# Forming the gate's token mixes in streams of their own, and loading them from DRAM in both halves

## The chip, the cores and the metric

The kernel runs on one core of one Trainium2 chip. The metric is the device time of one execution in microseconds (us). The time before is the median of three runs. A profile is one further execution, taken with the hardware profiler; it has its own time.

## The reference, cut to what matters

Two decoder layers work on 512 tokens of 1024 channels. Layer 0 is an RWKV-7 time mixing with a SiLU gate, layer 1 a differential attention; each ends with a small gated embedding. Only layer 0's input side matters here:

```
x_prev = jnp.pad(xn, ((0, 0), (1, 0), (0, 0)))[:, :-1]
xmix = xn[None] + (x_prev - xn)[None] * mu[:, None, None, :]
rkvg = jnp.einsum('cbsd,cde->cbse', xmix[:4], w_in)
r, k, v, g = rkvg[0], rkvg[1], rkvg[2], rkvg[3]
...
_, y = lax.scan(step, state0, (r, decay, k, v, kk, a))
...
y = y.reshape(B, S, D).astype(xn.dtype) * jax.nn.silu(g)
return y @ w_out
```

Each of r, k, v and the gate g has a mix of its own: the normalised tokens blended with the tokens shifted by one. The mix is multiplied with a 1024 x 1024 weight. r, k and v feed the scan; g is needed only behind it.

## The kernel before

**Tiles.** Channels lie on the 128 partitions in 8 tiles `d`. Every operand of a dense product is split in two float32r parts, high and low, and a product takes three matmuls of 128x512 (`mm3`, L284, L285 and L286: here called a triple). A weight of 1024x1024 is used in two halves `hf` of 512 output channels. One half of one projection (`dense_m`) is 8 tiles `d` by 4 output blocks `e`, so 32 triples. Weights arrive by DMA (`w_load`, two buffers RAW) and are split by `w_split`: a cast to the high part on ScalarE or VectorE (L269), a subtraction for the low part on GpSimd or VectorE (L317).

**Mixes.** The 8 mixes of a projection are formed from the resident x by `mix`: ScalarE scales x into PSUM (L529), VectorE adds the shifted token (L531), ScalarE casts the high part (L535), VectorE subtracts the low part (L537). ScalarE then issues a store of the mix to DRAM (`mD`, L541, 512 KB). The first half that uses a projection takes the mix as formed; the second half loads it from `mD` on SyncE's queue (L523). At most two mixes of each parity of `d` are held at once (`MT`).

**Order of the dense work.** `ORDER` runs the halves as r0, k0, v0, r1, k1, v1, p0, g0, g1, p1 (p is the layers' embedding). Thus the gate's mixes are formed when g0 is at hand, after v1.

**The recurrence.** The scan runs in chunks of 64 tokens, for two groups of heads (g = 0 and 1; eight chunks c each, `recur`). Ahead of it stand, for each group, Gram matrices (`gram`, L971 and L980) and, for each pair of chunks-of-128, a triangular inverse (`inverse`): 31 steps of a multiply and an add on VectorE (L1038, L1041), transposes (L1029, L1047, L1062), and two batches of 64 small matmuls (L1074, L1088). The recurrence itself is a chain TensorE, ScalarE or VectorE copy, TensorE (L1175, L1188, L1216), with the state's update on VectorE (L1228, L1231). Dense triples stand between these steps as filler. `finish` (L1259 and on) normalises a block and multiplies it with the gate; behind it layer 0's output projection `out0` begins.

**What sets the order.** The whole program is a set of Python generators ("streams"). A planner (`Streams`) runs them against a table of costs, priorities and buffer counts while the program is built, and so writes a fixed order of instructions for TensorE, VectorE, ScalarE and GpSimd. It also chooses the engine where a step names two. On the chip each engine runs its list in order, and waits where an operand isn't there. SyncE's queue issues its DMAs in the order in which the planner came to them. `R` is a ring of 4 KB buffers per partition, `H` one of 2 KB.

Of the kernel before, what the change touches and what calls it, by code (L numbers as in the profile page):

```python
# [8 lines left out]
F32 = mybir.dt.float32  # L9
F32R = mybir.dt.float32r  # L10
AF = mybir.ActivationFunctionType
ALU = mybir.AluOpType
# [3 lines left out]
P = 128  # L16
D = 1024
S = 512
NT = D // P
# [11 lines left out]
V_G, V_MU, V_W0, V_A0, V_KK, V_KA, V_LB, V_G1, V_GKV = 0, 1, 7, 8, 9, 10, 11, 12, 13  # L31
# [5 lines left out]
FIRST = [(k, h) for n, (k, h) in enumerate(ORDER) if k not in [x for x, _ in ORDER[:n]]]  # L37
# [3 lines left out]
N_WT, N_MT, N_RAW = 8, 2, 2  # L41
# [1 line left out]
WLP, WP = 6, 7  # L43
XLP = (6, 0.5)
LO2P = (3, 3)
MIXP = (4, 5)
DECP = (3, 3.5)
EVP = {"v": 1.5, "r": 4, "k": 3, "g": 3}
GRP, OPP, RECP, FINP = (5, 2.5), (4, 4), (0.3, 0.3), (7.5, 7.6)
# [152 lines left out]
def yoco_kernel(ctx: ExitStack, tc: tile.TileContext, I, out):  # L202
    nc = tc.nc
    k = Core(tc, ctx)
# [3 lines left out]
    def pool(name, bufs=1, **kw):  # L208
        return tc.tile_pool(name=name, bufs=bufs, **kw)

    dram = ctx.enter_context(pool("dram", space=bass.MemoryType.DRAM))
    N_R, N_H = 44 - N_RAW, 11
    gD = dram.tile([NT, P, S], F32, name="gD")
    vcD = dram.tile([NB, P, D], F32, name="vcD")
    hD = dram.tile([NB, P, D], F32, name="hD")
# [1 line left out]
    mD = dram.tile([4, NT, P, 2, S], F32, name="mD")  # L217
# [12 lines left out]
    def bank(tag):  # L230
        return T(pp, [P, 512], "p", bufs=8)

    def R(shape, dt=F32):
        return T(ring, shape, "R", dt, bufs=N_R)
# [4 lines left out]
    sc = Streams(dict(NBUF, R=N_R, H=N_H, WT=N_WT, RAW=N_RAW) | {("MT", par): N_MT for par in range(2)})  # L239
# [31 lines left out]
    def vcol(v, t):  # L271
        return vec[:, v, t : t + 1]
# [22 lines left out]
    def w_load():  # L295
        for key, src, _ in wants:
            yield "take", "RAW", 1
            RAW[key] = T(raws, [P, 2, S], "RAW", bufs=N_RAW)
            yield "DMA!", 1.7
            nc.sync.dma_start(RAW[key], src)  # L300
            yield "set", ("load",) + key

    def w_split():
        yield "wait", ("norms",)
        for key, _, scale in wants:
            yield "wait", ("load",) + key
            for u in range(2):
                yield "take", "WT", 1
                yield "take", "R", 1, True
                d = 2 * key[-1] + u  # L310
                f, t = RAW[key][:, u], R([P, 2, S], F32R)
                hi, lo = t[:, 0], t[:, 1]
                if scale is None:
                    yield "ACT/DVE+", (0.52, 0.34)
                    copy(hi, f)
                    yield "Pool+/DVE+!", (1.25, 0.6)
                    ENG[sc.eng].tensor_sub(lo, f, hi.bitcast(F32))  # L317
                else:
                    g = vcol(scale, d)
                    yield "ACT", 0.62  # L320
                    nc.scalar.activation(hi, f, AF.Copy, scale=g)  # L321
                    yield "DVE+!", 0.67
                    nc.vector.scalar_tensor_tensor(lo, f, g, hi.bitcast(F32), ALU.mult, ALU.subtract)  # L323
                W[key[:-1] + (d,)] = (hi, lo)
                yield "set", ("W",) + key[:-1] + (d,)
            yield "free", "RAW", 1
# [95 lines left out]
    MIX = {"r": 0, "k": 1, "v": 2, "g": 3}  # L422
# [83 lines left out]
    def x_at(d):  # L506
        return xh[d // 2][:, d % 2, :]

    mixes = {}

    def mix(key, hf, par):

        c = MIX[key]
        for d in range(par, NT, 2):
            yield "wait", ("xh", d)
            yield "take", ("MT", par), 1
            yield "take", "R", 1, True
            mixes[key, hf, d] = t = R([P, 2, S], F32R)
            h, l = t[:, 0], t[:, 1]
            if (key, hf) not in FIRST:  # L520
                yield "wait", ("kept", key, d)
                yield "DMA", 1.7
                nc.sync.dma_start(t.bitcast(F32), mD[c, d])  # L523
                yield "set", ("mix", key, hf, d)
                continue
            yield "take", "pw", 1
            m = bank("pw")
            yield "ACT", 0.57
            nc.scalar.activation(m, x_at(d), AF.Copy, scale=omm[:, c, d : d + 1])  # L529
            yield "DVE", 0.67  # L530
            nc.vector.scalar_tensor_tensor(  # L531
                m[:, 1:], x_at(d)[:, 0 : S - 1], vcol(V_MU + c, d), m[:, 1:], ALU.mult, ALU.add
            )
            yield "ACT", 0.48
            nc.scalar.copy(h, m)  # L535
            yield "DVE", 0.6
            nc.vector.tensor_sub(l, m, h.bitcast(F32))  # L537
            yield "free", "pw", 1
            yield "set", ("mix", key, hf, d)
            yield "ACT!", 0.06  # L540
            nc.scalar.dma_start(mD[c, d], t.bitcast(F32))  # L541
            yield "set", ("kept", key, d)

    def mix_all(par):
        for key, hf in MIXES:
            yield from mix(key, hf, par)
        yield "free", "R", 2


# [134 lines left out]
    omm = T(ax, [P, 4, NT], "omm")  # L684
# [227 lines left out]
        sc.add(lora2(g), LO2P[g])  # L912
    for par in range(2):
        sc.add(mix_all(par), MIXP[par])
    sc.add(w_load(), WLP)
    sc.add(w_split(), WP)
    sc.add(fill(), 8)
# [1053 lines left out]
```

## Time and profile before

| what | value |
|---|---|
| median of three runs | 807.28 us (805.05 to 807.47) |
| the profiled execution's own time | 804.08 us |
| its span in the trace | 802.3 us |
| TensorE busy | 757.8 us, 94% of the span |
| VectorE busy | 594.5 us, 74% |
| ScalarE busy | 460.1 us, 57% |
| GpSimd busy | 184.9 us, 23% |
| mean DMA rate | 180 GB/s |

The span is the time from the first to the last instruction in the trace; the remaining 1.78 us lie around it. Matmuls overlap and their ends are modelled, so a busy TensorE is not TensorE at its peak.

### The profile page before, as it was taken

To read this page: it belongs to the slowest core of one execution; us is meant where nothing else is said; L and a number is where in the kernel's file an instruction comes from. 1 tells how busy PE (TensorE), PEld (TensorE's weight loads), DVE (VectorE), ACT (ScalarE), POOL (GpSimd) and SP (SyncE) were. 2 spreads that over 40 slices of the span, in tenths; PEclk is the share of its full clock that TensorE was granted. 3 is DMA by queue.
4 is the path that set the end of the run, shared out by engine and by line. 5 is a ranking of instruction groups with operands and counts; after the bars stand their busy time and mean duration, and the time that the engine had idled before them with its cause. 6 is when DMAs were issued, how large, how long until landed. Compare 5 with 4: busy or idle time off the path is not lost.

```text
span 802.3 us, 13875 instructions
## 1 busy us (share of the span) xinstructions
PE 757.8 (94%) x5016; PEld 607.2 (76%) x5016; DVE 594.5 (74%) x1360; ACT 460.1 (57%) x1091; POOL 184.9 (23%) x208
## 2 busy tenths in 40 slices
PE   6898999997999869899999999999999999999996
PEld 3576678875778657788788888887888888888884
DVE  2999999987869798798767685456875668835844
ACT  3789754668747566766444565333764567743431
POOL 2416404422313303874301010000000002100000
PEclk9999999999999969999999999999999999999998
DMA  8586676822436646847257334588943434224702
GB/s 322 195 262 232 215 263 230 296 93 94 138 100 224 246 186 221 266 155 242 99 184 263 131 110 151 185 289 235 298 164 105 113 83 133 83 75 157 259 5 105
DMA packets 65525, 144.60 MB, mean 180 GB/s; under 512 B 6448, under 2 KB 27184, under 8 KB 65456
## 3 DMA queue, kind: packets, MB, share of 16 engines
q1 hardware_dynamic: 42672, 108.06, 40.3%
q10 hardware_dynamic: 22784, 35.66, 12.9%
q8 instruction: 39, 0.64, 0.3%
q14 instruction: 30, 0.25, 0.1%
HBM read 105.94 MB, written 37.75 MB: 179 GB/s over the span
## 4 chain that ended last, share of the span: by engine, by line
PE 70%; DVE 15%; ACT 7%; DMA 5%; issue 2%; SPq 0%; ACTq 0%; POOL 0%; DVEq 0%; POOLq 0%
PE p L284 17%; PE p L286 17%; PE p L285 16%; PE p L1175 3%; DVE p L1041 2%; PE p L1775 2%; PE p L1188 2%; DVE H L1038 2%; ACT R L269 2%; PE p L971 1%; DVE p L531 1%; PE p L1740 1%; PE p L1216 1%; DVE R L537 1%; PE p L1739 1%
## 5 line engine op out<-in xcount | busy, mean ns | idle before, releaser
L284 PE MATMUL p<-R,R 128*128 128x512 f32 x800 | 327.9, 410 | 6.8 <-ACT H L860 4.0
L285 PE MATMUL p<-R,R 128*128 128x512 f32 x800 | 314.2, 393 | 3.4 <-DVE R L537 3.4
L286 PE MATMUL p<-R,R 128*128 128x512 f32 x800 | 314.4, 393 | 0.0
L284 PEld LDWEIGHTS p<-R,R 128*128 128x128 f32 x800 | 151.2, 189 | 41.2 <-ACT H L860 5.2
L286 PEld LDWEIGHTS p<-R,R 128*128 128x128 f32 x800 | 151.1, 189 | 33.4 <-DVE R L1305 0.4
L285 PEld LDWEIGHTS p<-R,R 128*128 128x128 f32 x800 | 151.6, 190 | 31.8 <-DVE R L537 5.3
L317 POOL TENSOR_TENSOR R<-RAW,R 128x512 fp32r<-128x512 f32 x48 | 64.9, 1357 | 163.4 <-ACT R L269 119.5
L269 ACT CAST R<-RAW 128x512 fp32r<-128x512 f32 x110 | 65.8, 619 | 19.5 <-DMA RAW<-in_w_k 8.0
L317 DVE TENSOR_TENSOR R<-RAW,R 128x512 fp32r<-128x512 f32 x92 | 64.3, 710 | 12.1 <-ACT R L269 10.8
L323 DVE SCALAR_TENSOR_TENSOR R<-RAW,vec,R 128x512 fp32r<-128x512 f32 x64 | 46.6, 748 | 18.1 <-ACT R L321 17.8
L321 ACT ACTIVATE R<-RAW,vec 128x512 fp32r<-128x512 f32 x64 | 44.6, 720 | 19.3 <-DMA RAW<-in_b_w_in 12.6
L1751 ACT ACTIVATE H<-p,mx 128x128 f32<-128x128 f32 (+3 forms) x64 | 33.4, 528 | 19.9 <-DVE mx L1748 17.9
L1384 POOL TENSOR_TENSOR hr<-hm,half 128x1 f32<-128x1 f32 x16 | 10.4, 649 | 147.7 <-DVE hm L1382 147.7
L1744 DVE CUSTOM_DVE_ANT_0 p<-p,cmask 128x128 f32<-128x128 f32 (+3 forms) x64 | 31.2, 523 | 13.6 <-PE p L1740 13.3
L1041 DVE TENSOR_TENSOR p<-p,H 128x126 f32<-128x126 f32 (+22 forms) x124 | 32.6, 263 | 4.3
L280 POOL TENSOR_TENSOR orr<-orm,half 128x4 f32<-128x4 f32 x8 | 8.8, 1102 | 105.8 <-DVE orm L278 92.3
L1038 DVE TENSOR_TENSOR H<-p,R 128x126 f32<-128x126 f32 (+22 forms) x124 | 30.8, 248 | 1.3
L1521 DVE SCALAR_TENSOR_TENSOR R<-H,R 128x512 f32<-128x512 f32 x16 | 11.1, 691 | 24.3 <-ACT H L1514 22.5
L1514 ACT ACTIVATE H<-p 128x512 f32<-128x512 f32 x16 | 9.5, 596 | 31.0 <-PE p L286 31.0
L1443 ACT COPY R<-p 128x512 f32<-128x512 f32 x16 | 9.4, 588 | 30.9 <-PE p L286 30.8
L531 DVE SCALAR_TENSOR_TENSOR p<-R,vec,p 128x511 f32<-128x511 f32 x32 | 23.7, 748 | 4.5 <-ACT p L529 4.4
L529 ACT ACTIVATE p<-R,omm 128x512 f32<-128x512 f32 x32 | 22.1, 692 | 7.4 <-DVE R L980 2.0
(226 smaller groups left out, 1263.7 us busy)
## 6 DMA issues: line engine op xcount, KB each, us to landing
mD<-R ACTq DMA_DIRECT2D x32, 512.0 KB, 3.3
R<-mD SPq DMA_DIRECT2D x32, 512.0 KB, 5.7
RAW<-in_ple_gate SPq DMA_DIRECT2D x16, 512.0 KB, 3.7
RAW<-in_kv_w SPq DMA_DIRECT2D x16, 512.0 KB, 3.6
RAW<-in_b_w_in SPq DMA_DIRECT2D x16, 512.0 KB, 4.4
R<-bD ACTq DMA_DIRECT2D x24, 256.0 KB, 4.8
R<-in_x SPq DMA_DIRECT2D x8, 512.0 KB, 6.1
RAW<-in_w_r SPq DMA_DIRECT2D x8, 512.0 KB, 3.9
```

Of the source, the lines that this page charges most:

```text
L269: (nc.scalar.copy if sc.eng == "ACT" else ENG[sc.eng].tensor_copy)(dst, src)
L284: nc.tensor.matmul(ps, ah, bh, start=first, stop=False)
L285: nc.tensor.matmul(ps, ah, bl, start=False, stop=False)
L286: nc.tensor.matmul(ps, al, bh, start=False, stop=last)
L317: ENG[sc.eng].tensor_sub(lo, f, hi.bitcast(F32))
L321: nc.scalar.activation(hi, f, AF.Copy, scale=g)
L323: nc.vector.scalar_tensor_tensor(lo, f, g, hi.bitcast(F32), ALU.mult, ALU.subtract)
L531: nc.vector.scalar_tensor_tensor(m[:, 1:], x_at(d)[:, 0 : S - 1], vcol(V_MU + c, d), m[:, 1:], ALU.mult, ALU.add)
L1038: ve.tensor_mul(tmp[:, 0:m, 0:w], bc(xs[:, s_ : s_ + 1, 0:w], [P, m, w]), bc(nb[:, s_ + 1 : 32, s_ : s_ + 1], [P, m, w]))
L1041: ve.tensor_add(xs[:, s_ + 1 : 32, 0:w], xs[:, s_ + 1 : 32, 0:w], tmp[:, 0:m, 0:w])
L1744: nc.vector.tensor_tensor_reduce(scs[m][:, 0:n], scs[m][:, 0:n], cmask[:, S - n : S], 1.0, -3.0e38, ALU.add, ALU.max, mx[:, m : m + 1])
L1751: nc.scalar.activation(E[m][:, 0:n], scs[m][:, 0:n], AF.Exp, bias=mx[:, m : m + 1], scale=0.125, accum_out=sm[:, m : m + 1])
```

## The change

The first-half branch of `mix` becomes a function, `mixed`. For the projections in `AHEAD` (the gate alone) two new streams, `mix_ahead`, one for each parity of `d`, call it once the second half of the keys (k1) is done on TensorE. Each mix is formed in a ring buffer, stored to `mD`, and the buffer is given back; after the last one the place of x is given back as well, which `mix_all` no longer does. Both halves of g load their mixes from `mD`. The new streams have priority 6; the ring gains one buffer of 4 KB, and `H` loses two of 2 KB.

```
-MIXP = (4, 5)
+MIXP = (4, 5, 6)
+AHEAD = ("g",)
...
-    N_R, N_H = 44 - N_RAW, 11
+    N_R, N_H = 45 - N_RAW, 9
...
+    def mixed(key, d, t):
...
     def mix(key, hf, par):
...
-            if (key, hf) not in FIRST:
+            if key in AHEAD or (key, hf) not in FIRST:
                 yield "wait", ("kept", key, d)
                 yield "DMA", 1.7
-                nc.sync.dma_start(t.bitcast(F32), mD[c, d])
...
+                nc.sync.dma_start(t.bitcast(F32), mD[MIX[key], d])
+            else:
+                yield from mixed(key, d, t)
             yield "set", ("mix", key, hf, d)
...
     def mix_all(par):
         for key, hf in MIXES:
             yield from mix(key, hf, par)
+
+    def mix_ahead(par):
+
+        yield "wait", ("dense", "k", 1)
+        for key in AHEAD:
+            for d in range(par, NT, 2):
+                yield "take", "R", 1, True
+                yield from mixed(key, d, R([P, 2, S], F32R))
+                yield "free", "R", 1
         yield "free", "R", 2
...
     for par in range(2):
         sc.add(mix_all(par), MIXP[par])
+        sc.add(mix_ahead(par), MIXP[2])
```

The planner's order moves all over layer 0's first part. Three places follow. In the changed kernel the lines have other numbers: L521 and L525 are before's L531 and L537, L270 is L269, L1241 and L1244 are L1228 and L1231, L1051 and L1054 are L1038 and L1041, L285 to L287 are L284 to L286, L1188 is L1175.

VectorE, in the first group's recurrence, at the state's update of chunk 2 (`R_1691`), before: keys' steps stand ahead of it and the keys' norms behind.

```order
L866 TENSOR_TENSOR R_1840<-H_2109,R_1840 128x4x2x64
L868 TENSOR_TENSOR R_1475<-H_2109,R_1475 128x4x128
L1228 TENSOR_TENSOR R_1691<-R_1691,p_2119 64x4x64
L1231 TENSOR_TENSOR R_1691<-R_1691,pcall_99 64x4x64
L1228 TENSOR_TENSOR R_1691<-R_1691,p_2119 64x4x64
L1231 TENSOR_TENSOR R_1691<-R_1691,pcall_99 64x4x64
L722 SCALAR_TENSOR_TENSOR R_1840<-H_2109,der_96,R_1840 128x4x128
```

The same place in the changed kernel (the state is `R_1716`, the gate's mixes read x from `R_116` and `R_118`):

```order
L521 SCALAR_TENSOR_TENSOR p_2114<-R_116,vec_87,p_2114 128x511
L521 SCALAR_TENSOR_TENSOR p_2124<-R_116,vec_87,p_2124 128x511
L1241 TENSOR_TENSOR R_1716<-R_1716,p_2135 64x4x64
L525 TENSOR_TENSOR R_1994<-p_2114,R_1994 128x512
L1244 TENSOR_TENSOR R_1716<-R_1716,pcall_99 64x4x64
L1241 TENSOR_TENSOR R_1716<-R_1716,p_2135 64x4x64
L1244 TENSOR_TENSOR R_1716<-R_1716,pcall_99 64x4x64
L525 TENSOR_TENSOR R_1995<-p_2124,R_1995 128x512
L521 SCALAR_TENSOR_TENSOR p_2200<-R_118,vec_87,p_2200 128x511
```

All 16 VectorE steps of the gate's mixes now stand from just ahead of chunk 2's update to just behind chunk 5's in the first group's recurrence.

VectorE, at the end of the second group's first inverse (`p_2586`) and the start of its second (`p_3050`), before:

```order
L1041 TENSOR_TENSOR p_2586<-p_2586,H_2579 128x16
L531 SCALAR_TENSOR_TENSOR p_3157<-R_167,vec_87,p_3157 128x511
L1047 STREAM_TRANSPOSE R_3172<-p_2586 128x1024
L1029 STREAM_TRANSPOSE R_3186<-H_3005 128x1024
L1058 SCALAR_TENSOR_TENSOR H_3180<-R_3172,rowm_104,H_3180 128x32x16
L1038 TENSOR_TENSOR H_3007<-p_3050,R_3186 128x31
```

The same in the changed kernel (the two inverses are `p_2776` and `p_3010`): the second begins while the first still has 13 steps to go, and no mix is among them.

```order
L1042 STREAM_TRANSPOSE R_3123<-H_2993 128x1024
L1051 TENSOR_TENSOR H_2758<-p_2776,R_2895 128x13x10
L1054 TENSOR_TENSOR p_2776<-p_2776,H_2758 128x13x10
L1051 TENSOR_TENSOR H_2995<-p_3010,R_3123 128x31
L1054 TENSOR_TENSOR p_3010<-p_3010,H_2995 128x31
L1051 TENSOR_TENSOR H_2758<-p_2776,R_2895 128x12x10
L1054 TENSOR_TENSOR p_2776<-p_2776,H_2758 128x12x10
```

All eight L531 and L537 of the gate stood among the second group's Gram matrices and inverses; now the two inverses alternate there.

TensorE, at the first matmuls of the second group's recurrence (L1175), before. The triples are those of the gate's first half, tile d = 7 (mix `R_3253`, weight `R_3037`); the first of its four blocks stands ahead.

```order
L286 MATMUL p_2994<-R_3131,R_2981 128x512
L284 MATMUL p_2933<-R_3253,R_3037 128x512
L285 MATMUL p_2933<-R_3253,R_3037 128x512
L286 MATMUL p_2933<-R_3253,R_3037 128x512
L1175 MATMUL p_3382<-R_2637,R_2467 64x64 x2
L1175 MATMUL p_3382<-R_2637,R_2468 64x64 x2
```

The same in the changed kernel: the triples are those of the gate's second half, tile d = 2 (mix `R_3274`, weight `R_3162`).

```order
L287 MATMUL p_3390<-R_3243,R_3152 128x512
L285 MATMUL p_3311<-R_3274,R_3162 128x512
L286 MATMUL p_3311<-R_3274,R_3162 128x512
L287 MATMUL p_3311<-R_3274,R_3162 128x512
L1188 MATMUL p_3486<-R_2755,R_2567 64x64 x2
L1188 MATMUL p_3486<-R_2755,R_2568 64x64 x2
```

Counted over the whole list, 237 triples stand ahead of this place before and 249 now. At the last matmul of the second group's recurrence the counts are 296 and 305. From the output projection on, the list of TensorE is nearly the same in both.

## Rows read from the trace of the kernel before

**Rows 1.** The page: span, busy time and share by engine, granted clock in 40 slices.

```profile
span 802.3 us, 13875 instructions
...
PE 757.8 (94%) x5016; PEld 607.2 (76%) x5016; DVE 594.5 (74%) x1360; ACT 460.1 (57%) x1091; POOL 184.9 (23%) x208
...
PEclk9999999999999969999999999999999999999998
```

**Rows 2.** Windows by stretch: length, busy PE, PEld, DVE, ACT, POOL; PEclk, DMA, GB/s.

```profile
172.00:245.00 73.00, 67.36 (x834) 52.26 (x832) 56.30 (x108) 50.99 (x137) 17.09 (x26) 0.98 0.32 104
244.50:308.50 64.00, 53.45 (x421) 41.78 (x422) 56.50 (x161) 42.16 (x98) 18.45 (x19) 0.89 0.61 218
308.50:383.00 74.50, 72.39 (x842) 57.66 (x839) 63.26 (x134) 45.34 (x119) 46.26 (x50) 1.00 0.68 220
383.00:470.00 87.00, 86.70 (x405) 71.03 (x405) 62.28 (x111) 44.77 (x94) 10.84 (x12) 1.00 0.47 162
470.00:802.00 332.00, 322.54 (x1614) 269.85 (x1612) 208.43 (x527) 165.84 (x420) 31.09 (x33) 0.99 0.48 153
```

**Rows 3.** Waits of TensorE, 244.5 to 308.5 us: us in total, times, longest.

```profile
PE p L1074 <- DVE H L1062: 5.0, 1, 5.0
PE p L971 <- DVE R L537: 2.9, 1, 2.9
```

**Rows 4.** Waits of VectorE, 172 to 245 us.

```profile
DVE H L269 <- ACT H L269: 5.3, 3, 3.1
DVE R L866 <- ACT H L860: 2.9, 1, 2.9
```

**Rows 5.** Groups by line, 240.5 to 300 us: busy us, mean ns, idle before.

```profile
L531 DVE SCALAR_TENSOR_TENSOR p<-R,vec,p 128x511 f32<-128x511 f32 x8 | 6.0, 748 | 4.0 <-ACT p L529 4.0
...
L537 DVE TENSOR_TENSOR R<-p,R 128x512 fp32r<-128x512 f32 x8 | 5.5, 681 | 0.0
...
L535 ACT CAST R<-p 128x512 fp32r<-128x512 f32 x8 | 4.7, 587 | 6.1 <-DVE p L531 5.9
```

**Rows 6.** Timeline of TensorE, first and last recurrence steps of the second group.

```profile
302.00 0.86 PE L1175 MATMUL p<-R,R 128*64 128x64 f32 x16
...
382.15 0.69 PE L1175 MATMUL p<-R,R 128*64 128x64 f32 x16
```

**Rows 7.** Windows: r's second half, g's first half, a dense stretch; columns as Rows 2.

```profile
121.40:145.40 24.00, 24.00 (x121) 19.68 (x121) 22.86 (x78) 10.20 (x28) 11.89 (x13) 1.00 0.78 272
261.70:306.80 45.10, 34.55 (x295) 26.64 (x294) 38.59 (x112) 28.69 (x75) 10.51 (x10) 0.85 0.57 209
500.00:520.00 20.00, 20.00 (x90) 16.53 (x89) 9.30 (x14) 5.56 (x10) 0.95 (x1) 1.00 0.52 180
```

**Rows 8.** Groups by line, whole run: the weights' low part on GpSimd and VectorE.

```profile
L317 POOL TENSOR_TENSOR R<-RAW,R 128x512 fp32r<-128x512 f32 x48 | 64.9, 1357 | 163.4 <-ACT R L269 119.5 <-issue 28.7 <-DVE R L269 3.9
...
L317 DVE TENSOR_TENSOR R<-RAW,R 128x512 fp32r<-128x512 f32 x92 | 64.3, 710 | 12.1 <-ACT R L269 10.8
```

**Rows 9.** Groups by line, 172 to 245 us: small copies on VectorE.

```profile
L269 DVE COPY H<-p 64x256 f32<-64x256 f32 x4 | 1.7, 425 | 5.6 <-ACT H L269 5.3 <-PE p L1188 0.3
...
L269 DVE COPY H<-R 32x128 f32<-32x128 f32 x6 | 1.3, 216 | 0.1
```

**Rows 10.** Tile mD, 100 to 160 us: loads of mixes and time to landing.

```profile
L523 SPq DMA_DIRECT2D R<-mD x15: 319/422/562, 106.7 to 153.2; - x15
...
DMA to landing us min/median/max: 2.7/5.8/8.6
```

**Rows 11.** Line L1231, the state's update: duration ns min/median/max.

```profile
L1231 DVE TENSOR_TENSOR R<-R,pcall x24: 409/422/1340, 176.2 to 376.7; 64x256 f32<-64x256 f32 x24
```

More of the change, by code (lines that the diff above doesn't have):

```diff
@@ L509, in yoco_kernel @@
     mixes = {}
+    def mixed(key, d, t):
+        c = MIX[key]
+        h, l = t[:, 0], t[:, 1]
+        yield "take", "pw", 1
+        m = bank("pw")
+        yield "ACT", 0.57
+        nc.scalar.activation(m, x_at(d), AF.Copy, scale=omm[:, c, d : d + 1])
+        yield "DVE", 0.67
+        nc.vector.scalar_tensor_tensor(m[:, 1:], x_at(d)[:, 0 : S - 1], vcol(V_MU + c, d), m[:, 1:], ALU.mult, ALU.add)
+        yield "ACT", 0.48
+        nc.scalar.copy(h, m)
+        yield "DVE", 0.6
+        nc.vector.tensor_sub(l, m, h.bitcast(F32))
+        yield "free", "pw", 1
+        yield "set", ("mixed", key, d)
+        yield "ACT!", 0.06
+        nc.scalar.dma_start(mD[c, d], t.bitcast(F32))
+        yield "set", ("kept", key, d)
     def mix(key, hf, par):
-        c = MIX[key]
         for d in range(par, NT, 2):
@@ L518, in mix @@
             mixes[key, hf, d] = t = R([P, 2, S], F32R)
-            h, l = t[:, 0], t[:, 1]
-            if (key, hf) not in FIRST:
+            if key in AHEAD or (key, hf) not in FIRST:
                 yield "wait", ("kept", key, d)
                 yield "DMA", 1.7
-                nc.sync.dma_start(t.bitcast(F32), mD[c, d])
[L524 to L538, printed above, removed]
+                nc.sync.dma_start(t.bitcast(F32), mD[MIX[key], d])
+            else:
+                yield from mixed(key, d, t)
             yield "set", ("mix", key, hf, d)
-            yield "ACT!", 0.06
-            nc.scalar.dma_start(mD[c, d], t.bitcast(F32))
-            yield "set", ("kept", key, d)
     def mix_all(par):
```

## The prediction

> **What bounds the kernel now.** I read the page first: TensorE is busy 94% of the span and its granted clock dips in one slice out of 40, the fifteenth (280 to 300 us) [rows 1]. A busy share over the whole run hides where the rest lies, so next came the windows by stretch [rows 2]. The reader is to see three things there. From 383 us on TensorE is busy 86.70 of 87.00 us and then 322.54 of 332.00: what follows layer 0's recurrence is TensorE's own work, and a change ahead of it is kept if TensorE reaches that point sooner. From 244.5 to 308.5 us, where the gate's mixes are formed and the second group's inverses run, TensorE is busy only 53.45 of 64.00 us, at a granted 0.89, so part of it at the lower of the two levels, 1.2 instead of 2.4 GHz. VectorE is busy 56.50 of those 64.00 us. From 172 to 245 us, the first group's recurrence, VectorE is busy only 56.30 of 73.00 us, and TensorE 67.36.
>
> The waits say who is waited for. From 244.5 to 308.5 us TensorE waits 5.0 us for the inverse's transpose (L1062) and 2.9 us for L537, the last step of a mix [rows 3]. All eight of the gate's mixes are formed there: on VectorE 8 x 0.748 + 8 x 0.681 = 11.4 us, of which only one step waited, 4.0 us, for ScalarE [rows 5]. So in this stretch VectorE's list sets the time; TensorE has nothing else to do, since the dense work it could do (the gate's halves) waits for the mixes in that same list. From 172 to 245 us VectorE waits instead, mostly for the recurrence's chain: 5.3 us for copies on ScalarE, 2.9 us for the keys' steps [rows 4].
>
> The same dense work with loaded mixes stands in the trace: r's second half takes its 32 triples in 24.00 us with TensorE busy all the time. The gate's first half takes 45.10 us, TensorE busy 34.55 [rows 7]. Not all of the difference is the mixes' doing (the inverses' and the recurrence's matmuls lie in it too), but 10.55 us of idle TensorE are.
>
> **The change part by part.** I count up to one point, T: the last matmuls of the second group's recurrence, at 382.15 us, which began at 302.00 [rows 6]. Behind T the list of TensorE is nearly the same, so the time changes by the shift of T, less the work that TensorE has by then done in advance.
>
> *Work done in advance.* At T the new list has 305 triples behind it, the old 296. A triple at full clock takes 20.00 / 30 = 0.667 us (90 matmuls in the 20 us of the dense stretch [rows 7]). Nine triples are 6.0 us less to do after T. This is sure if T doesn't move.
>
> *VectorE's list up to T.* The mixes are in it in both kernels, so they cancel. The planner now gives GpSimd 11 more of the weights' subtractions: 11 x 0.710 = 7.8 us less on VectorE [rows 8]. It gives VectorE 17 more of the inverses' small copies, 17 x 0.216 = 3.7, and takes back six copies of 64x256, 6 x 0.425 = 2.6 [rows 9]. A few steps of finish and casts that stand on the other side of T, counted the same way, make +1.1. Net: 5.6 us less.
>
> *Idle VectorE that the mixes may fill.* They leave a stretch with 64.00 - 56.50 = 7.5 us of idle VectorE for one with 73.00 - 56.30 = 16.7 us [rows 2]. What they fill there pulls everything behind forward, the Gram matrices and the inverses first. At best all 11.4 us; at worst none, because a list is run in order: a mix that stands in front of a chunk's update delays the chain even when the update's operand is there. The new order puts them right among the updates of chunks 2 to 5. I take 3 us, nearer the lower end, since the waits there are in short pieces.
>
> *Loading the mixes for g0.* Eight more loads of 512 KB. Such loads land 5.8 us after issue in the median [rows 10] and are issued up to two tiles ahead for each parity; r's second half ran with them at 272 GB/s without an idle moment on TensorE [rows 7]. The cover is the queue of dense triples, 2.7 us for each tile. Without it the cost would be at most 24.00 - 32 x 0.667 = 2.7 us. I take 0. On SyncE's queue a load of tile 4 or later waits until TensorE is done with the tile four before it, and the weights' loads and the gate's stores stand behind it; r's second half ran with the same rule. The eight stores of the mixes move forward into 172 to 245 us, where the DMA share is 0.32 instead of 0.61 [rows 2]: 0 too.
>
> *What is new or late.* GpSimd has more to do up to T, 13 subtractions, 13 x 1.357 = 17.6 us [rows 8]; it is busy 18.45 of 64.00 and 46.26 of 74.50 us in the two stretches ahead of T [rows 2], so it fits, but finish's steps stand behind them in its list. The recurrence of the second group is a chain of round trips between engines: with VectorE's list shorter it will not shrink by the whole amount. From its first step to T the list holds 56 triples instead of 59, so TensorE's own work there falls only by 2.0 us. For both I give back 2.5 us; bounds 0 and all of the 5.6.
>
> *Two fewer buffers of H, one more of R.* Hidden as long as VectorE and ScalarE keep up with TensorE in the last 400 us; the bound is taken at 2 us, a fifth of TensorE's 9.5 us of idle time in 470 to 802 us [rows 2]. I take 0.
>
> **Sum.** -6.0 - 5.6 - 3.0 + 2.5 = -12.1 us. Against the profiled execution, 802.3 us of span and 1.8 around it, 804.1 in all, that is 792.0. The median of the runs shown is 807.28, 3.2 higher, so a median of the changed kernel should be 795. The other side's check: TensorE has 5.6 + 10.6 us of idle time in the two stretches, and at most 64 x 0.11 = 7 us of full-clock work lost to the lower level, part of it in the same idle time. That makes some 20 us the most that can be won, 787.
>
> One rule of the Trainium skill speaks against the move to GpSimd. The state's update takes 0.409 us at its shortest and 1.340 at its longest [rows 11]; something holds it up by as much as 0.93 us. The Trainium skill ("SBUF — State Buffer", Who interferes with whom) says why: a VectorE instruction with two inputs in SBUF and a GpSimd instruction that reads SBUF take the same port as a lock, and the later one blocks. By that rule 13 more GpSimd subtractions would cost VectorE up to 12 us; what that does is the third rival.
>
> **The rivals.**
> 1. *The chain keeps its pace.* The second group's recurrence starts at 302 and ends at 382 as before, paced by its round trips; then only the nine triples are won, 6.0 us: 801 on the median's scale. For it: eight chunks in 80.2 us, while VectorE is busy 63.26 of 74.50 [rows 2, 6]. Against it: 85% busy leaves little room for a chain that waits for nothing but itself.
> 2. *Nothing is filled.* The first group's recurrence is longer by all of the mixes' 11.4 us, and the later stretch gets back nothing for it beyond the first two terms: 804.1 - 6.0 - 5.6 + 11.4 = 803.9, the median 807: no change. Against it: up to the first group's last chunk the two lists of VectorE differ by 7.6 us, not 11.4.
> 3. *GpSimd blocks VectorE.* 13 subtractions, each holding up a VectorE step by as much as 0.93 us [rows 11]: 12.1 us, which eats the gain: 807. Against it: nearly all inverse steps read one operand from PSUM (`p`), and the largest delay is one of 24.
> 4. *Slower: the mixes stall VectorE's list.* A mix goes back and forth between ScalarE and VectorE, L529, L531, L535, L537; where ScalarE is late VectorE's whole list stands, and the updates of chunks 2 to 5 with it. One of the eight stood 4.0 us before [rows 5]. From 12.1 / 8 = 1.5 us for each mix the gain is gone; if four of eight stand as long as that one it is 792.0 + 4 x 4.0 = 808.0, the median 811. Against it: the other seven waited nothing, and ScalarE is busy 50.99 of 73.00 us there.
>
> **How the numbers follow.** A run of this kernel can tell some 0.3%, 2.4 us, from no change. The forecast (a gain of 8 to 20 us): 0.57. The first rival (3 to 8 us): 0.24. No change, by the second or third: 0.10. Slower, by the fourth: 0.09. Faster is thus 0.81, the same 0.10, slower 0.09. The likeliest case gives 795, its own range 787 to 799. The range that holds the time 8 times in 10 must take in the first rival and the small end of the gain, up to 805; below, 784, for the bounds of the filled time and of the clock together.
>
> **What would show it.** Right: the gate's 32 triples in about 25 us instead of 45; no mix among the inverses' steps; a granted clock near 1.00 in 280 to 300 us or a shorter dip; VectorE's idle time in the first group's recurrence below 16.7 us; T at 376 us or before, with TensorE busy behind it as now. Wrong: T at 382 or later; first chunks 2 to 6 of the first group spread by more than 8 us, with VectorE waiting at L521 or L525 for ScalarE; updates of the state at over 1 us in number; TensorE waiting for loads of `mD` in g0.

## Result and profile after

The changed kernel takes 797.02 us (median of four, 795.49 to 800.16) against 807.38 us for the kernel before on the same chip (805.05 to 808.0): a ratio of 0.9892, 95% interval 0.9867 to 0.9917. That is 6.7 to 10.7 us less, 8.7 by the ratio itself: a gain of 1.1%, clear of the noise, and inside the range. (That goes by the recorded ratio; the two medians alone lie 10.4 us apart.) The profiled execution took 797.09 us.

The page, as [rows 1]: span and engines, then the granted clock in 40 slices.

```profile
span 795.3 us, 13941 instructions
...
PE 756.1 (95%) x5016; PEld 605.1 (76%) x5016; DVE 589.8 (74%) x1360; ACT 454.5 (57%) x1078; POOL 201.9 (25%) x221
...
PEclk9999999998999899999999999999999999999998
```

The dip to 6 tenths is gone; two slices stand at 8, 179 to 199 us and 258 to 278 us. The windows by stretch, in the columns of [rows 2], with 383 to 430 us apart and the gate's first half (as in [rows 7]) last:

```profile
172.00:245.00 73.00, 67.74 (x826) 52.32 (x826) 56.04 (x109) 58.19 (x146) 24.97 (x33) 0.95 0.55 188
244.50:308.50 64.00, 58.84 (x481) 46.40 (x479) 57.34 (x174) 32.71 (x83) 23.46 (x22) 0.95 0.67 233
308.50:383.00 74.50, 72.62 (x822) 58.04 (x823) 67.99 (x125) 45.15 (x120) 46.24 (x48) 1.00 0.55 180
383.00:430.00 47.00, 43.13 (x205) 34.76 (x205) 34.18 (x60) 21.24 (x45) 5.34 (x6) 1.00 0.56 188
470.00:795.00 325.00, 316.04 (x1582) 264.67 (x1580) 202.40 (x516) 160.59 (x410) 27.55 (x30) 0.99 0.47 151
...
261.39:290.39 29.00, 25.88 (x113) 21.07 (x112) 24.79 (x87) 13.34 (x30) 12.70 (x10) 0.88 0.76 268
```

Two things stand out. In the stretch of the inverses TensorE idles 64.00 - 58.84 = 5.16 us instead of 10.55, at a clock of 0.95 instead of 0.89: the gate's first half takes 29.0 us, not 45.1. And from 383 to 430 us it idles 3.87 us; before it was busy 46.70 of these 47.00 us. Part of the gain is given back there.

What TensorE waits for, 244.5 to 308.5 us (as [rows 3]) and then 383 to 430 us:

```profile
PE p L984 <- ACT H L1501: 3.1, 1, 3.1
PE p L1087 <- DVE H L1075: 1.6, 1, 1.6
...
PE p L1410 <- DVE R L1469: 2.2, 1, 2.2
PE p L285 <- DVE R L270: 1.7, 1, 1.7
```

The wait for a mix's last step is gone, and that for the inverse's transpose (L1075, before L1062) fell from 5.0 to 1.6 us. New are the embedding's evacuation on ScalarE (L1501), which a Gram matmul (L984) waits for, and, behind the recurrence, the end of the layer (L1469). The wait for the weights' cast (L270, before L269) grew from 0.3 to 1.7 us.

The second group's recurrence on TensorE, timeline, as [rows 6]:

```profile
301.00 0.69 PE L1188 MATMUL p<-R,R 128*64 128x64 f32 x16
...
378.44 0.69 PE L1188 MATMUL p<-R,R 128*64 128x64 f32 x16
```

The transpose of a finished block in `finish` (ns min/median/max, first and last start in us), line L1304 after and then L1291 before:

```profile
L1304 PE MATMUL p<-ident,R x32: 272/273/329, 325.7 to 387.1; 128*128 128x128 f32 x32
```

```profile
L1291 PE MATMUL p<-ident,R x32: 270/272/273, 340.7 to 396.0; 128*128 128x128 f32 x32
```

The recurrence starts 1.0 us earlier (302.00) and T comes 3.7 us earlier (382.15). I call the last start of that transpose F: it moved by 8.9 us, from 396.0 to 387.1. From F to the end of the span it is 406.3 us before and 408.2 after.

Up to F TensorE idles 34.4 us before and 26.1 after, 8.3 less, nearly all of the 8.9. By stretch: 2.3 us less ahead of 172 us, 0.4 in 172 to 244.5 us, 5.4 among the inverses, 0.2 behind. The first part lies ahead of all the gate's mixes (on VectorE from 192.7 us on), most of it in one place (windows before and then after):

```profile
60.00:100.00 40.00, 35.04 (x177) 25.06 (x177) 37.80 (x64) 34.39 (x65) 22.07 (x19) 0.96 0.63 224
```

```profile
60.00:100.00 40.00, 36.76 (x186) 25.75 (x185) 37.15 (x65) 35.19 (x66) 26.12 (x22) 1.00 0.60 222
```

### The profile page after: what moved, and what is told of

It reads as the page before. It is cut to its first block, busy times and chain, and to the rows that moved or that the text cites. A ratio compares the mean times of both kernels' runs of the same rounds, so it can differ in the third digit from the quotient of the medians.

```text
span 795.3 us, 13941 instructions
## 1 busy us (share of the span) xinstructions
PE 756.1 (95%) x5016; PEld 605.1 (76%) x5016; DVE 589.8 (74%) x1360; ACT 454.5 (57%) x1078; POOL 201.9 (25%) x221
## 4 chain that ended last, share of the span: by engine, by line
PE 70%; DVE 8%; ACT 8%; DMA 8%; issue 2%; POOL 2%; SPq 1%; ACTq 0%; POOLq 0%; DVEq 0%
PE p L285 18%; PE p L287 18%; PE p L286 18%; PE p L1788 2%; PE p L984 2%; PE p L1188 2%; ACT R L270 1%; PE p L1753 1%; PE p L1752 1%; PE p L1201 1%; DMA R<-bD 1%; PE p L1779 1%; DMA RAW<-in_ple_w 1%; PE p L1410 1%; DMA R<-mD 1%
## 5 line engine op out<-in xcount | busy, mean ns | idle before, releaser
L285 PE MATMUL p<-R,R 128*128 128x512 f32 x800 | 326.4, 408 | 3.2 <-DVE R L270 1.7
L286 PE MATMUL p<-R,R 128*128 128x512 f32 x800 | 314.1, 393 | 3.8 <-DVE R L525 3.6
L287 PE MATMUL p<-R,R 128*128 128x512 f32 x800 | 314.4, 393 | 0.0
L285 PEld LDWEIGHTS p<-R,R 128*128 128x128 f32 x800 | 151.3, 189 | 37.1 <-DVE R L270 1.9
L287 PEld LDWEIGHTS p<-R,R 128*128 128x128 f32 x800 | 151.0, 189 | 33.2 <-DVE R L1318 0.4
L286 PEld LDWEIGHTS p<-R,R 128*128 128x128 f32 x800 | 151.5, 189 | 32.4 <-DVE R L525 4.9
L318 POOL TENSOR_TENSOR R<-RAW,R 128x512 fp32r<-128x512 f32 x59 | 78.6, 1339 | 163.3 <-ACT R L270 89.1
L270 ACT CAST R<-RAW 128x512 fp32r<-128x512 f32 x110 | 66.1, 619 | 26.7 <-DMA RAW<-in_w_g 10.0
L318 DVE TENSOR_TENSOR R<-RAW,R 128x512 fp32r<-128x512 f32 x81 | 56.8, 715 | 11.0 <-ACT R L270 10.2
L1397 POOL TENSOR_TENSOR hr<-hm,half 128x1 f32<-128x1 f32 x16 | 10.4, 648 | 147.2 <-DVE hm L1395 147.2
L1054 DVE TENSOR_TENSOR p<-p,H 128x126 f32<-128x126 f32 (+22 forms) x124 | 32.6, 263 | 4.3
L1051 DVE TENSOR_TENSOR H<-p,R 128x126 f32<-128x126 f32 (+22 forms) x124 | 30.5, 246 | 1.1
L521 DVE SCALAR_TENSOR_TENSOR p<-R,vec,p 128x511 f32<-128x511 f32 x32 | 23.5, 747 | 5.4 <-ACT p L519 5.3
L1788 PEld LDWEIGHTS p<-R,H 128*128 128x128 f32 x160 | 22.1, 191 | 2.8 <-ACT H L1805 0.5
```

The lines of the kernel that those rows point to most:

```text
L270: (nc.scalar.copy if sc.eng == "ACT" else ENG[sc.eng].tensor_copy)(dst, src)
L285: nc.tensor.matmul(ps, ah, bh, start=first, stop=False)
L286: nc.tensor.matmul(ps, ah, bl, start=False, stop=False)
L287: nc.tensor.matmul(ps, al, bh, start=False, stop=last)
L1051: ve.tensor_mul(tmp[:, 0:m, 0:w], bc(xs[:, s_ : s_ + 1, 0:w], [P, m, w]), bc(nb[:, s_ + 1 : 32, s_ : s_ + 1], [P, m, w]))
L1054: ve.tensor_add(xs[:, s_ + 1 : 32, 0:w], xs[:, s_ + 1 : 32, 0:w], tmp[:, 0:m, 0:w])
```

## The experiments

The theories after the result. **A**: the gain is that VectorE's list between the two recurrences loses the gate's mixes, so that TensorE gets its triples. **B**: the buffers (one more of R, two fewer of H) carry it. **L**: any edit gives the planner's order a new shape, and the gain is one draw of it. Each run's time stands beside runs of the kernel before on its own chip (medians 805.15, 805.35 and 806.15 us in the three groups of four), so the ratios are what can be compared.

**1 and 2: each half of the change alone.** e1 is the kernel before with the new buffer counts, e2 the changed kernel with the old ones.

```
# e1, in before            # e2, in the changed kernel
-N_R, N_H = 44 - N_RAW, 11 -N_R, N_H = 45 - N_RAW, 9
+N_R, N_H = 45 - N_RAW, 9  +N_R, N_H = 44 - N_RAW, 11
```

> The kernel before with the changed kernel's buffer counts alone (45 in the ring R in place of 44, 9 of H in place of 11). The gate's mixes are still formed among the second group's inverses; the planner's order nevertheless has 303 triples ahead of T instead of 296 (the changed kernel 305). Theory A (the gain comes from taking the mixes out of VectorE's list in that stretch): T moves later by most of what the seven triples win, 803 to 807 us. Rival B (the buffers, which also set x's place and the planner's order, carry the gain): 797 to 801 us.

> The changed kernel with the old buffer counts (44 of R, 11 of H): the new streams and loads alone. Its order has 309 triples ahead of T. Theory A: all of the gain or a little more (four triples at 0.667 us are 2.7 us), 794 to 799 us. Rival B (the buffers carry it): 803 to 808 us.

Both are slower than before: e1 815.66 us, ratio 1.0132 [1.0107, 1.0157]; e2 809.81 us, 1.0056 [1.0035, 1.0078]. Rival B falls, and so do A's numbers: e1 is 9 us above its range, e2 11. Windows of e1 and then of e2, 244.5 to 308.5 and 383 to 430 us:

```profile
244.50:308.50 64.00, 52.58 (x377) 41.05 (x375) 54.03 (x139) 38.32 (x96) 20.69 (x20) 0.89 0.59 198
383.00:430.00 47.00, 40.95 (x238) 32.26 (x235) 33.93 (x65) 16.21 (x37) 10.03 (x9) 0.96 0.41 134
```

```profile
244.50:308.50 64.00, 56.38 (x430) 44.44 (x425) 56.20 (x172) 35.17 (x89) 25.59 (x25) 0.95 0.76 262
383.00:430.00 47.00, 42.26 (x232) 33.79 (x231) 33.92 (x60) 19.73 (x44) 8.79 (x9) 0.96 0.44 143
```

In the inverses' stretch they go as A says: with the mixes there TensorE idles 11.4 us, without them 7.6. But from 383 to 430 us e1 idles 6.05 us and e2 4.74 us, and both reach F later than before (405.8 and 398.2 against 396.0). More triples ahead of T did not help: e1 has seven more than before and e2 thirteen, and T came at 392.8 and 390.3 us by the last matmul's start, against 382.6.

**3 and 4: the mixes' price at either place, with the order frozen.** The planner still sees the steps, so the order stays; the four instructions of each of the gate's mixes, and its store, are not emitted. Both halves of the gate load r's mixes instead, which in e3 adds eight loads.

```
 # e3 in mix of before, e4 in mixed of the changed kernel; the same for all four steps
             yield "DVE", 0.67
+            if key != "g":
                 nc.vector.scalar_tensor_tensor(m[:, 1:], ...)
```

> The kernel before, its order of instructions frozen, with the four steps of each of the gate's eight mixes left out (the gate's halves are fed r's mixes from DRAM, so the gate's values are not the reference's). VectorE's list is 11.4 us shorter in the stretch of the second group's inverses. Theory A (VectorE's list sets the time there): 6 to 11 us less, 796 to 801 us. Rival C (the stretch is paced by the inverses' own round trips and TensorE; the mixes only fill gaps): 0 to 3 us less, 804 to 807 us.

> The changed kernel, order frozen, with the same steps left out (same note on the gate's values). VectorE's list is 11.4 us shorter in the first group's recurrence. Theory A as put on record (about 3 of the 11.4 us were filled there, the rest lengthens that recurrence): the recurrence of the first group ends 5 to 8 us earlier, and the time falls by 4 to 8 us, to 789 to 793 us. Rival D (what the mixes cost there is made up behind them, since TensorE has dense triples to do meanwhile): 0 to 2 us, 795 to 797 us.

e3: 801.58 us, ratio 0.9959 [0.9941, 0.9976]: 3.3 us less (1.9 to 4.8), at rival C's edge. TensorE's idle time among the inverses falls from 10.6 to 6.9 us. The second group's recurrence starts at 296.55 instead of 302.00, so of the 11.4 us of VectorE's work 5.4 stood in the way there, and 2 of these were lost again behind. e4: 794.40 us, ratio 0.9861 [0.9834, 0.9889]; the changed kernel's own is 0.9892 [0.9867, 0.9917], on another chip. That is 2.5 us less, between the two ranges, and the intervals overlap; it lies nearer to rival D. The last state update of the first group (timeline of VectorE) in the changed kernel, then in e4:

```profile
238.00 0.42 DVE L1244 TENSOR_TENSOR R<-R,pcall 64x256 f32<-64x256 f32 x1
```

```profile
234.71 0.42 DVE L1249 TENSOR_TENSOR R<-R,pcall 64x256 f32<-64x256 f32 x1
```

The mixes lengthen the first recurrence by 3.3 us; about 8 of their 11.4 us are filled. So with the order of before as it is, taking the mixes' work out is worth 3.3 us, less than half of the 8.7 that the change gained. The two runs side by side say more: on one chip, with the gate's mixes in neither and the same loads in both, e4 is still 7.2 us faster than e3. Most of the gain thus lies in the order and the buffers, not in the time that the mixes themselves take.

**5 and 6: another place for the mixes.** One line of the changed kernel:

```
-        yield "wait", ("dense", "k", 1)
+        yield "wait", ("dense", "v", 1)   # e5
+        yield "wait", ("dense", "r", 1)   # e6
```

> The changed kernel, with the mixes formed by their own streams only once the second half of the values (v1) is done instead of the keys' (k1). They stand on VectorE between the first group's last state update and the second group's first one again, among the inverses, as in the kernel before; streams, stores, loads for both halves and buffer counts are the changed kernel's. What counts is the stretch from the end of the first group's recurrence to the start of the second's (63.1 us before, 57.5 us changed, 58.0 us before without the mixes). Theory A, narrowed (the gain is that VectorE's list in that stretch loses the mixes): 62 to 65 us there, the median 801 to 807 us. Rival B (the loads, streams and buffers do it, wherever the mixes stand): as the changed kernel, 795 to 799 us.

> The changed kernel with the mixes formed once r's second half is done (r1), one projection earlier: they stand on VectorE ahead of the first group's recurrence and in its first two chunks. The order has 314 triples ahead of T instead of 305, and 2 instead of 11 between T and the last block's normalisation on TensorE. My prediction's rule (each triple ahead of T is 0.667 us won): 6 us faster than the changed kernel, 790 to 792 us. Theory F (what counts is when the last block's normalisation is done, and the cover behind T only moves TensorE's wait): no gain from these triples, 797 to 805 us.

e5: 808.36 us, 1.0041 [1.0020, 1.0061]; e6: 813.06 us, 1.0097 [1.0068, 1.0125]. Neither B nor the rule of triples ahead of T survives. In e5, the window of the inverses' stretch, and TensorE's first wait there:

```profile
244.50:308.50 64.00, 45.38 (x371) 34.55 (x371) 48.46 (x137) 34.53 (x83) 19.57 (x23) 0.86 0.79 280
```

```profile
PE p L285 <- DMA R<-mD: 15.2, 3, 9.9
```

The mixes are formed late, and then go to DRAM and back before TensorE can use them: 18.6 us idle, 15.2 of them on loads of `mD`. The first mix's store was issued at 254.0 us, its load landed at 266.0, and TensorE, idle for 9.9 us, went on at 266.1. The stretch between the two recurrences took 69.8 us, more than A had said. In e6 the windows show that stretch full, but not the rest; the line behind them is TensorE's longest wait, 383 to 430 us:

```profile
172.00:244.50 72.50, 62.20 (x768) 48.39 (x766) 55.04 (x100) 49.45 (x122) 20.16 (x31) 0.86 0.43 149
244.50:308.50 64.00, 62.05 (x543) 49.16 (x539) 57.63 (x181) 40.83 (x106) 17.99 (x18) 1.00 0.65 226
...
383.00:430.00 47.00, 38.70 (x251) 30.81 (x252) 31.07 (x62) 17.53 (x42) 11.36 (x11) 0.93 0.29 98
```

```profile
PE p L1304 <- DVE R L1293: 4.9, 1, 4.9
```

The mixes delay the first recurrence, and behind T only two triples are left to cover `finish`: TensorE waits 4.9 us for it at one point and idles 8.3 us in all from 383 to 430 us. Theory F's range (797 to 805) is passed too, since F itself came at 402.1 us.

**7 to 12: the same work in other orders.** The planner prefers an engine for a step by `PREF = 0.15` us. Other values leave the work alone and change the order and, for some steps, the engine.

```
-PREF = 0.15
+PREF = 0.16   # e7 before, e8 changed, e11 as e2, e12 as e1
+PREF = 0.14   # e9 before, e10 changed
```

> The kernel before, with the planner's preference between two engines for a step changed from 0.15 to 0.16 us, which means nothing by itself; its order of VectorE's list differs in many places (304 triples ahead of T instead of 296). Theory A (the place of the mixes decides): within 0.5% of before, 802 to 810 us. Rival L (any new order moves the time, and the change's gain is one draw of it): anything from 795 to 816 us.

> The changed kernel with the same 0.16 instead of 0.15; its order differs too, less widely. Theory A: within 0.5% of the changed kernel, 793 to 801 us. Rival L: anything from 795 to 816 us; above 802 us the gain would hang on the order that came out.

> The kernel before with the planner's preference at 0.14 us, a third order of the same work (305 triples ahead of T). So far the order of before and two others with the mixes among the inverses gave 807, 816 and 815 us, all three with TensorE idle 10.6 to 11.8 us in 244.5 to 308.5 us. Theory A: the idle time there again 9 to 13 us; the total by what stands behind T, 803 to 817 us. Rival L (orders scatter, and the place of the mixes shows in no stretch): idle there anywhere from 5 to 18 us.

> The changed kernel with the preference at 0.14 us, a third order of it (304 triples ahead of T). Theory A: TensorE idle 4 to 9 us in 244.5 to 308.5 us, the median 793 to 803 us. Rival L: as wide as before's three orders, up to 810 us.

> The changed kernel with the old buffer counts (44 of R, 11 of H) and the preference at 0.16 us; with 0.15 it took 809.8 us. If the one buffer of R is what the mixes ahead need (theory B2): 805 to 814 us again. If that run was one poor order (rival L): 795 to 803 us.

> The kernel before with the changed kernel's buffer counts and the preference at 0.16 us; with 0.15 it took 815.7 us. Theory A: TensorE idle 9 to 13 us in 244.5 to 308.5 us and 803 to 817 us. If the buffers could carry the gain in another order (rival B): below 801 us.

All whole runs, by where the gate's mixes stand. Idle is the window less TensorE's busy time; "done" counts the triples that TensorE has started when the second recurrence starts. In most orders T comes after 383 us, so the last column holds the end of the recurrence too. Times in us.

| run | R/H, PREF | median | ratio [95%] | idle 244.5-308.5 | 2nd recurrence from | done | F | idle 383-430 |
|---|---|---|---|---|---|---|---|---|
| *among the inverses* | | | | | | | | |
| before | 44/11, .15 | 807.38 | 1 | 10.6 | 302.0 | 237 | 396.0 | 0.3 |
| e9 | 44/11, .14 | 806.03 | 1.0006 [0.9985, 1.0026] | 13.2 | 300.2 | 240 | 395.8 | 2.2 |
| e7 | 44/11, .16 | 814.71 | 1.0118 [1.0095, 1.0141] | 11.8 | 301.4 | 240 | 403.2 | 5.9 |
| e1 | 45/9, .15 | 815.66 | 1.0132 [1.0107, 1.0157] | 11.4 | 308.0 | 237 | 405.8 | 6.1 |
| e12 | 45/9, .16 | 803.57 | 0.9962 [0.9934, 0.9990] | 11.5 | 299.5 | 238 | 395.3 | 2.5 |
| *ahead (from k1 on)* | | | | | | | | |
| changed | 45/9, .15 | 797.02 | 0.9892 [0.9867, 0.9917] | 5.2 | 301.0 | 249 | 387.1 | 3.9 |
| e10 | 45/9, .14 | 807.45 | 1.0027 [1.0001, 1.0054] | 7.7 | 300.7 | 246 | 396.5 | 4.7 |
| e8 | 45/9, .16 | 797.12 | 0.9901 [0.9880, 0.9922] | 8.2 | 305.5 | 251 | 389.2 | 2.8 |
| e2 | 44/11, .15 | 809.81 | 1.0056 [1.0035, 1.0078] | 7.6 | 309.2 | 249 | 398.2 | 4.7 |
| e11 | 44/11, .16 | 809.97 | 1.0058 [1.0027, 1.0090] | 5.4 | 307.1 | 249 | 398.4 | 3.1 |
| *later (v1)*: e5 | 45/9, .15 | 808.36 | 1.0041 [1.0020, 1.0061] | 18.6 | 304.2 | 236 | 400.1 | 1.7 |
| *earlier (r1)*: e6 | 45/9, .15 | 813.06 | 1.0097 [1.0068, 1.0125] | 2.0 | 305.8 | 249 | 402.1 | 8.3 |

A is shown in its own stretch: five orders with the mixes among the inverses idle 10.6 to 13.2 us there, five with the mixes ahead 5.2 to 8.2, and the latter have done 246 to 251 triples by the second recurrence instead of 237 to 240. It is not shown in the total. Orders of the same work differ by 1.7% (0.9962 to 1.0132 with the mixes among the inverses, 0.9892 to 1.0058 with them ahead), more than the change. The means of the five are 1.0044 and 0.9987: 0.57% apart, with a standard error of 0.51% worked out from the scatter within each. e10 holds the changed kernel's code with another tie constant and wins nothing. A's times for e7 and e10 fail, e9's idle time is just past A's 13 us, and L's "in no stretch" fails too.

The five orders of either kind mix the buffer counts. The change as it was made (code and buffers together) is, at 0.14, 0.15 and 0.16, 0.2% slower, 1.1% faster and 2.2% faster than before: 1.0% in the mean, with a standard error of 0.6%. One part of the gain does come in every order: in 60 to 100 us TensorE idles 3.2 to 3.3 us in all seven orders of the changed code and 5.0 to 5.5 in the five of the code before. Which line of the change does that was not tested.

Where e10 loses it is seen in its windows beside those of the changed kernel:

```profile
172.00:244.50 72.50, 64.56 (x781) 49.74 (x779) 61.86 (x108) 55.22 (x134) 28.26 (x34) 1.00 0.54 183
244.50:308.50 64.00, 56.29 (x495) 43.96 (x492) 58.02 (x160) 33.69 (x93) 24.79 (x26) 0.89 0.77 257
308.50:383.00 74.50, 72.81 (x840) 58.47 (x841) 66.37 (x134) 43.26 (x116) 37.40 (x42) 0.95 0.47 153
383.00:430.00 47.00, 42.32 (x223) 33.72 (x222) 32.88 (x62) 21.28 (x47) 7.09 (x7) 1.00 0.45 142
```

It is no single place: 2.7 us more idle in 172 to 244.5 (the changed kernel is busy 67.24 of these 72.50), 2.6 among the inverses, 0.8 from 383 to 430 us, and a lower clock in two stretches (0.89 and 0.95 instead of 0.95 and 1.00), a higher one in the first (1.00 instead of 0.95).

With the old buffer counts both orders with the mixes ahead lose (e2, e11), as theory B2 said; their second recurrence starts at 309.2 and 307.1 us. Whether the one ring buffer does that, or the two orders share a poor piece, was not told apart.

## Why the prediction was right, and where its steps were wrong

The median, 797.02, is 2 us from the forecast, but two errors cancel in that. On the scale of the profiled execution the sum gave 792.0 and 797.09 was measured, so the gain of 12.1 was 7.0. The 3.2 us that I added for the median was not there after the change: its profiled execution lies at its median.

- *Work done in advance, -6.0.* The count was right, nine triples. The condition, "if T doesn't move", was the weak step. From 308.5 to 383 us TensorE is busy 72.62 of 74.50 us, so from the recurrence's first step to T the time goes with the triples that stand in between (54 in e8: 74.7 us; 65 in e6: 88.9 us), and a triple put there pushes T out. e2 (13 more than before) and e6 (18 more) reached T 7.7 and 12.1 us later. In every order 314 to 316 triples stand ahead of F; what a change can win is TensorE's idle time and slow clock up to F, not triples ahead of a point. For the changed kernel the two ways of counting happen to agree: -6.0 - 3.7 = -9.7 at T, -8.9 at F.
- *VectorE's list, filling and give-back, -5.6 - 3.0 + 2.5 = -6.1.* T moved by 3.7. The term that failed is the list, -5.6: up to T VectorE is busy 323.43 us before and 322.97 after, 0.5 less (windows from 0 to the last matmul of T, before and then after).

```profile
0.00:382.62 382.62, 348.22 (x3000) 266.05 (x3000) 323.43 (x724) 249.34 (x577) 142.58 (x163) 0.97 0.60 209
```

```profile
0.00:378.91 378.91, 352.85 (x3031) 269.21 (x3031) 322.97 (x725) 248.56 (x572) 164.79 (x179) 0.98 0.64 223
```

  Up to T VectorE lost 9 of the weights' subtractions (43 to 34), not 11. The 17 more small copies came, but cost 8.2 us, not 3.7 (groups by line in the same windows, two of before and two of after):

```profile
L269 DVE COPY R<-H 32x128 f32<-32x128 f32 x13 | 2.8, 217 | 0.3
L269 DVE COPY H<-R 32x128 f32<-32x128 f32 x12 | 2.6, 213 | 0.1
```

```profile
L270 DVE COPY R<-H 32x128 f32<-32x128 f32 x22 | 7.8, 356 | 0.4
L270 DVE COPY H<-R 32x128 f32<-32x128 f32 x20 | 5.8, 290 | 0.3
```

  Six of the 42 took 0.86 to 1.01 us instead of 0.22, and each of the six began while GpSimd was inside a 128x512 step: 4.4 us in all. What moved T is VectorE's idle time, 59.2 us up to T before and 55.9 after, 3.3 of the 3.7 us. The filling, -3.0, was thus about right. By e4 some 8 of the mixes' 11.4 us are filled at the new place, but by e3 6 were filled at the old one already: e3 took 11.4 us out and the recurrence started 5.4 us earlier, so that VectorE's list "sets the time" among the inverses held for half.
- *Behind T "the list of TensorE is nearly the same": 0.* This step failed. With fewer triples behind T, 11 instead of 18 up to `finish`'s last transpose, TensorE reaches the output projection's weights and the end of the layer before they are ready: 3.87 us idle instead of 0.30. That is read from the waits. The price differs with the order, 0.3 to 8.3 us in the table, and the number of triples alone does not set it: e5 with 18 idles 1.7 us, e1 with 13 6.1.
- *Loads for g0: 0.* Right: TensorE has no wait for `mD` among the inverses. In e2 it has 1.5 us of them from 172 to 309 us; e5 shows the price where the store and the load follow each other at once.
- *Fewer H buffers: 0.* From 470 us on TensorE idles 325.00 - 316.04 = 8.96 us, as before (9.46).

The signs named ahead: no mix among the inverses came. The gate's half took 29.0 us, not 25: the Gram matmul behind its first two triples waited 3.1 us for L1501, and the clock there was 0.88. VectorE's idle time in 172 to 245 us didn't fall (16.96 us): a fixed window doesn't show filling when the work in it shifts. T at 378.44 missed "376 or before". Two signs of being wrong came near: from chunk 2's update to chunk 6's in the first group it is 41.8 us instead of 34.4 (7.4 more, where 8 was named), and 5 of the 24 updates of [rows 11] took over 1 us instead of 2.

The rivals. The first had a real core: the chain's start moved by 1.0 us only. Nothing filled: refuted by e4 and by VectorE's idle time up to T. The slower one, VectorE waiting for ScalarE inside the mixes, is there, but small (waits of VectorE, 172 to 245 us):

```profile
DVE H L270 <- ACT H L270: 4.4, 2, 3.4
DVE p L521 <- ACT p L519: 4.1, 4, 1.8
```

4.1 us over eight mixes is 0.5 each, where 1.5 would have eaten the gain. GpSimd's block of VectorE, the third: the state's update, as [rows 11], went from a mean of 0.539 to 0.633 us over its 24 instances, 2.3 us in all. With the 4.4 us of the six copies that is 6.7 us, over half of the rival's 12.1: it had a real core too, and took about what the list was to lose. VectorE's other steps weren't summed.

```profile
L1244 DVE TENSOR_TENSOR R<-R,pcall x24: 407/422/1280, 177.6 to 372.0; 64x256 f32<-64x256 f32 x24
```

So the direction was right and the mechanism is seen among the inverses, but the sum came near by luck (its list term was nearly all wrong), and "faster" rested on an order whose neighbours range from 1.0% faster (e8) to 0.6% slower (e2, e11). No probability for that stood among my rivals. The best order found is the changed kernel itself; e8 equals it.

## What to carry to other kernels

Where a planner writes the order, a change of code is also a new draw of the order: run two or three orders of either kernel (a tie constant will do) before a gain near 1% is put down to the idea. Count what is won as the idle time of the busiest engine up to a point behind which every order holds the same work, not as work moved ahead of a point that can itself move. A detour through DRAM was free here with the last store issued at 230.7 us and its half begun at 261.4 us (the changed kernel), and cost 15.2 us of TensorE's time with store and load next to each other (e5). When steps are moved to another engine, price what that engine then does to its neighbour as well.

## What was unexpected of the hardware

VectorE's and GpSimd's hold on each other shows plainly in e2. Three subtractions of weights on VectorE take 3.59 us, 1.20 each, where the mean of this step in the changed kernel is 0.72 us; beside them GpSimd runs from 384.35 to 387.29 us (timelines of VectorE and then GpSimd in e2, then the three subtractions' ns min/median/max).

```profile
384.24 3.59 DVE L318 TENSOR_TENSOR R<-RAW,R 128x512 fp32r<-128x512 f32 x3
```

```profile
384.35 1.48 POOL L1272 TENSOR_TENSOR R<-R,vmean 128x512 f32<-128x512 f32 x1
385.92 1.37 POOL L1274 TENSOR_TENSOR R<-R,bon 128x512 f32<-128x512 f32 x1
```

```profile
L318 DVE TENSOR_TENSOR R<-RAW,R x3: 692/1527/1531, 384.2 to 386.3; 128x512 fp32r<-128x512 f32 x3
```

The first, which began 0.11 us ahead of GpSimd's step, took 0.69 us; the other two, begun while GpSimd was at work, 1.53 each, and either ended 0.54 us after the GpSimd step that it met. The Trainium skill ("SBUF — State Buffer", Who interferes with whom) states a lock on a shared port for such a pair, where the second to issue blocks until the first is done; the trace agrees, and the two held steps lost 1.7 us here. The updates of [rows 11], a product of two operands, say the same: in the changed kernel all eight that took over 0.6 us, and before all five, began while GpSimd was inside a 128x512 step. How much it costs hangs on where the two lists happen to meet: GpSimd got 13 more subtractions, yet of the six slow copies only one met a subtraction (L318); the others met L662, L1272 and L1274.
